# Three seven-product pairs as third, fifth and seventh of eight, a bank emptied twice, and banks that swap in odd blocks

## The chip, the cores and the metric

The kernel runs on one core of a Trainium2 chip. The time is device microseconds of one execution of the whole program; lower is better. In the profile PE is TensorE's matmuls, PEld its weight loads, DVE is VectorE, ACT is ScalarE, POOL is GpSimd, and SP issues most of the DMAs.

## What is computed

Two transformer-like blocks run on 256 tokens of width 2048, in float32. The changed part is the feed-forward half of the first block: a normalised input is multiplied by a matrix of 2048 x 11264 whose left half gives `g` and whose right half gives `u`, and `silu(g) * u` is multiplied by a matrix of 5632 x 2048.

```python
h2 = _rmsnorm(x, ffn_norm_w[l])
g, u = jnp.split(jnp.einsum('bsd,df->bsf', h2, w_gate_up[l]), 2, axis=-1)
x = x + jnp.einsum('bsf,fd->bsd', jax.nn.silu(g) * u, w_down[l])
```

## The kernel before

**Three matmuls for one product.** Every float32 operand is split into a high and a low part of a shorter float type (`parts_of` for weights: ScalarE writes `wh`, VectorE writes `wl = raw - wh`). `tri` (L642) makes a product from three matmuls of 128x128 by 128x512 at L645, L646 and L647: high by high, high by low, low by high.

**Blocks and pairs.** `hidden_pre(f, ...)` works on one block f of 512 columns of `g` and the 512 columns of `u` that belong to it; there are 11 blocks, done in parts of 4, 4 and 3, and each part is followed by its share of the down product (`proj(gu, w_down, ...)`, matmuls at L166 to L168). Inside a block the 2048 rows of the weight are eight pairs p of 2 x 128 rows. The tokens are two tiles of 128, so a pair is a 2x2 by 2x2 product of tiles (tokens by rows, rows by `g`/`u`). A *plain* pair makes its eight products. A *seven-product* pair makes seven, from sums of tiles: the sums of the inputs (`F`, four of them) are made once, by `seven_forms`, for the pairs in `sums7`; the sums of the weights (`Ta`, `Tb`) are made by VectorE for each block and pair (L687 to L691), and they are split like the weights. Before the change the pairs 2, 4 and 7 are of this kind.

**Banks.** There are eight banks for matmul results. Five are the pool `pmm` (tile name p in the profile, `mm_bank`), three are the pool `phd` (tile name h, `bank`). A block holds all eight: P1, P2, P5, P6, P7 in `pmm` and P3, P4, X4 in `phd`. Plain pairs write P2, P4 (the `g` half, two token tiles), P3 and X4 (the `u` half). Seven-product pairs write P1, P2, P5, P7, P6, P4 and P3, in that order. X4 gets nothing from a seven-product pair, so before the last pair it is copied out (`x4`, L679), and `before_last` runs the *turn* of the previous block in it: eight transposes (L735) that turn the previous block's hidden values, in two halves of four, each read by ScalarE and VectorE (`unit_split`). A pool gives its buffers in rotation: the tile asked for next waits until the readers of the one that had the buffer are done.

**Emptying.** After the last pair the seven banks are combined (L715 to L723): `s1` is a copy of P1; then eight additions on VectorE, of which each reads at most one bank. Two Silu on ScalarE and two multiplications on VectorE (`hd`, L725 and L726) end the block.

**Loads and order.** A load is 512 KB (`load`, L115), issued by SP into the ring of `raw` buffers, two pools of four used in turn. `Ta` and `Tb` are taken from the same ring. Split weights live in six buffer pairs (`more_w`). The framework sorts the instructions of each engine beforehand, by readiness and priority; loads, splits, weight sums and the emptying have a raised priority (`tc.high_priority`). At run time each engine goes through its list in order. So a block's matmuls don't stand in the list in the order of the source.

Of the kernel before, what the change touches and what calls it, by code (L numbers as in the profile page):

```python
# [8 lines left out]
F32 = mybir.dt.float32  # L9
# [4 lines left out]
ALU = mybir.AluOpType  # L14
# [5 lines left out]
NT = 2  # L20
CW = 512
# [8 lines left out]
def tile_two_blocks(  # L30
# [19 lines left out]
    def stt(out, in0, scalar, in1, op0, op1):  # L50
        nc.vector.scalar_tensor_tensor(out=out, in0=in0, scalar=scalar, in1=in1, op0=op0, op1=op1)  # L51

    def tt(out, a, b, op):
        nc.vector.tensor_tensor(out=out, in0=a, in1=b, op=op)  # L54
# [7 lines left out]
    def act(out, in_, func=AF.Copy, **kw):  # L62
        nc.scalar.activation(out=out, in_=in_, func=func, **kw)  # L63
# [4 lines left out]
    def bank(shape):  # L68
        return phd.tile(shape, F32, tag="h", name="h")
# [38 lines left out]
    def raw_tile(nk, n):  # L108
        raw = (more_raw[-1] if more_raw else wraw).tile([128, nk, n], F32, tag="raw", name="raw")
        more_raw.reverse()  # L110
        return raw

    def load(w, r0, nk, c0, n):
        raw = raw_tile(nk, n)
        nc.sync.dma_start(  # L115
            out=raw, in_=w[r0:r0 + nk * 128, c0:c0 + n].rearrange("(k p) n -> p k n", p=128)
        )
        return raw

    def parts_of(raw, pool=None):  # L120
        if pool is None:
            pool = more_w[0] if more_w else wsp
            if more_w:
                more_w.append(more_w.pop(0))
        wh = pool.tile(list(raw.shape), F32R, tag="wh", name="wh")
        wl = pool.tile(list(raw.shape), F32R, tag="wl", name="wl")
        act(wh, raw)
        tt(wl, raw, wh.bitcast(F32), ALU.subtract)
        return wh, wl

    def split(w, r0, nk, c0, n, pool=None):
        with tc.high_priority(4000):
            return parts_of(load(w, r0, nk, c0, n), pool)

    def mm_bank():
        return pmm.tile([128, CW], F32, tag="p", name="p")
# [6 lines left out]
    def ordered(a):  # L143
        return a.rearrange("p (b h) -> p h b", h=2)

    def two(a):
        return a.rearrange("p (h b) -> p h b", h=2)
# [122 lines left out]
    def col(name, k):  # L270
        o = off[name] + k
        return cm[:, o:o + 1]
# [328 lines left out]
    fp = ff.enter_context(tc.tile_pool(name="fp", bufs=1))  # L601
    sums7 = {}

    def seven_forms(c):

        def keep(j, ps):
            p = 2 * c + j
            if p not in (2, 4, 7):
                return
            x_ = fp.tile([128, CW], F32, tag="s1", name="xs").rearrange("p (a t) -> p a t", a=2)  # L610
            for a in range(2):
                act(x_[:, a], ps[:, a], scale=col("ffn", 2 * p + a))
            (a11, a21), (a12, a22) = ((x_[:, a, :128], x_[:, a, 128:]) for a in range(2))
            s_ = fp.tile([128, CW], F32, tag="u2", name="ss").rearrange("p (i t) -> p i t", i=4)
            tt(s_[:, 0], a21, a22, ALU.add)
            tt(s_[:, 1], s_[:, 0], a11, ALU.subtract)
            tt(s_[:, 2], a11, a21, ALU.subtract)
            tt(s_[:, 3], a12, s_[:, 1], ALU.subtract)
            F = fp.tile([128, 4, 2, 128], F32R, tag=f"F{p}", name=f"F{p}")
            act(F[:, :, 0], s_)  # L620
            tt(F[:, :, 1], s_, F[:, :, 0].bitcast(F32), ALU.subtract)
            sums7[p] = F
        return keep
# [18 lines left out]
    def tri(pt, left, right, st, sp):  # L642
        (xh, xl), (wh, wl) = left, right
        mh, ml = in_turn(wh), in_turn(wl)
        nc.tensor.matmul(pt, lhsT=xh, rhs=mh, start=st, stop=False)  # L645
        nc.tensor.matmul(pt, lhsT=xh, rhs=ml, start=False, stop=False)  # L646
        nc.tensor.matmul(pt, lhsT=xl, rhs=mh, start=False, stop=sp)  # L647

    def hidden_pre(f, before_last):

        P1, P2, P6, P7, P5 = [mm_bank() for i in range(5)]
        P3, P4, X4 = [bank([128, CW]) for i in range(3)]
        begun = set()
        order = [0, 1, 2, 3, 4, 5, 6, 7]
        last_plain = max(p for p in order if p not in sums7)

        def prod(pt, left, right, end=False):
            tri(pt, left, right, id(pt) not in begun, end)
            begun.add(id(pt))

        for p in order:
            u, a0 = x1u[p // 2], 2 * (p % 2)
            r0, end = 256 * p, p == order[-1]

            def x_(a, t):
                sl = slice(t * 128, (t + 1) * 128)
                return u[:, a0 + a, 0, sl], u[:, a0 + a, 1, sl]

            if p not in sums7:
                for (b0, b1), c0 in (((P2, P4), f * CW), ((P3, X4), DFF + f * CW)):  # L670
                    wh, wl = split(w_gate_up, r0, 2, c0, CW)
                    for a in range(2):
                        for t, b in enumerate((b0, b1)):
                            prod(b, x_(a, t), (wh[:, a], wl[:, a]), b is X4 and p == last_plain and a == 1)
                continue
            if end:
                x4 = fp.tile([128, CW], F32, tag="x4", name="x4")
                with tc.high_priority(4000):
                    act(x4, X4)  # L679
                before_last(X4)  # L680
            F = sums7[p]
            with tc.high_priority(4000):
                g_ = load(w_gate_up, r0, 2, f * CW, CW)
                u_ = load(w_gate_up, r0, 2, DFF + f * CW, CW)
                B1 = parts_of(g_)
                Ta, Tb = raw_tile(2, CW), raw_tile(2, CW)
                tt(Ta[:, 0], u_[:, 0], g_[:, 0], ALU.subtract)  # L687
                tt(Ta[:, 1], u_[:, 1], u_[:, 0], ALU.subtract)
                W13 = parts_of(Ta)
                tt(Tb[:, 0], u_[:, 1], Ta[:, 0], ALU.subtract)  # L690
                tt(Tb[:, 1], g_[:, 1], Tb[:, 0], ALU.subtract)  # L691
                W24 = parts_of(Tb)
                B22 = parts_of(u_[:, 1:2])

            def at(w, a):
                return w[0][:, a], w[1][:, a]

            def form(i):
                return F[:, i, 0], F[:, i, 1]

            prod(P1, x_(0, 0), at(B1, 0), end)
            prod(P2, x_(1, 0), at(B1, 1), end)
            prod(P5, form(0), at(W13, 0), end)
            prod(P7, form(2), at(W13, 1), end)
            prod(P6, form(1), at(W24, 0), end)
            prod(P4, x_(1, 1), at(W24, 1), end)
            prod(P3, form(3), at(B22, 0), end)

        s1 = fp.tile([128, CW], F32, tag="s1", name="s1")
        u2 = fp.tile([128, CW], F32, tag="u2", name="u2")  # L710
        u3 = fp.tile([128, CW], F32, tag="u3", name="u3")
        g = fp.tile([128, NT, CW], F32, tag="g", name="g")
        h = fp.tile([128, NT, CW], F32, tag="hd", name="hd", bufs=2)
        with tc.high_priority(4000):
            act(s1, P1)  # L715
            tt(g[:, 0], P2, s1, ALU.add)
            tt(u2, P6, s1, ALU.add)
            tt(u3, P7, u2, ALU.add)
            tt(g[:, 1], P4, u3, ALU.add)
            tt(u2, P5, u2, ALU.add)  # L720
            tt(u3, P5, u3, ALU.add)
            tt(u2, P3, u2, ALU.add)
            tt(u3, u3, x4, ALU.add)  # L723
        for t, up_ in enumerate((u2, u3)):
            act(g[:, t], g[:, t], AF.Silu, scale=rs1[:, t:t + 1])  # L725
            stt(two(h[:, t]), ordered(up_), rs1[:, t:t + 1], ordered(g[:, t]), ALU.mult, ALU.mult)  # L726
        return h
# [16 lines left out]
    for part in (range(0, 4), range(4, 8), range(8, 11)):  # L744
        gu = []
        waiting = lambda ps: None
        for f in part:
            h = hidden_pre(f, waiting)
            gu.append((new_unit(), f * CW))
            waiting = turn(h, gu[-1][0])  # L750
        waiting(bank([128, CW]))
        for c in range(4):
            residual(proj(gu, w_down, c * CW), c)
            if part[-1] == 10:
                x2u.append(unit_from(xk(c), lambda k, c=c: wfg[:, 4 * c + k:4 * c + k + 1]))
                stats_piece(st, xc(c), c)
# [294 lines left out]
    for t in range(NT):  # L1051
        sl = slice(t * 128, (t + 1) * 128)
        n = CW if t == 0 else CW // 2
# [64 lines left out]
```

## Time and profile before

| | us |
|---|---|
| median of three executions | 1635.47 |
| lowest, highest | 1633.23, 1636.78 |
| the profiled execution | 1633.28 |
| its span | 1631.5 |
| gate/up blocks and down product, first to last matmul | about 523 to 1227 |

Matmul rows overlap: the time of a row is longer than the distance to the next one. So a stall is read from the distance between starts, or by counting matmuls in a window. Transposes of the turn are the rows `h<-ident,hd`; the products of a seven-product pair that use a sum of inputs are the rows with `F` among their operands; in the emptying the names are `s` (`s1`), `u` (`u2`, `u3`), `g` and `x` (`x4`).

### The profile page before, as it was taken

What the parts mean: (1) busy time and instruction counts of PE and PEld (TensorE: products, weight loads), DVE (VectorE), ACT (ScalarE), POOL (GpSimd) and SP (SyncE); (2) the same over time, 40 slices, a digit from 0 to 9 for tenths busy, and PEclk for the clock granted to TensorE, in tenths of its full rate; (3) what the DMA queues carried; (4) which work ended last, traced back from release to release, by engine and by line L of the source; (5) the groups of instructions that cost most, each with busy time, mean ns of one, the idle gap of its engine ahead of it and who ended that gap; (6) DMA issues with size and microseconds to landing.
All of it is one profiled execution on the core that took longest, in us unless ns stands there. A gap on an engine that the chain in (4) does not pass through costs nothing.

```text
span 1631.5 us, 22403 instructions
## 1 busy us (share of the span) xinstructions
PE 1596.9 (98%) x8433; PEld 1410.5 (86%) x8433; DVE 1238.2 (76%) x1715; ACT 885.5 (54%) x1156; POOL 23.6 (1%) x57
## 2 busy tenths in 40 slices
PE   8999999999999999999999999998999999999998
PEld 7999999999988888788887788887889888998987
DVE  7769768765667798875699875688877899766854
ACT  5657557544555555554455554455545455655743
POOL 3000000000000000000000000000000000000000
PEclk9999999999999999999999999999999999999999
DMA  8764565466686566675665576465856566556564
GB/s 291 216 196 153 156 191 168 146 191 197 218 285 204 169 201 189 210 248 171 195 197 185 186 251 209 147 201 184 261 170 186 176 182 218 183 166 192 159 216 143
DMA packets 166892, 318.36 MB, mean 195 GB/s; under 512 B 12248, under 2 KB 13168, under 8 KB 166784
## 3 DMA queue, kind: packets, MB, share of 16 engines
q1 hardware_dynamic: 164304, 312.19, 61.2%
q10 hardware_dynamic: 2032, 4.60, 0.8%
q8 instruction: 66, 1.08, 0.3%
q0 software_dynamic: 448, 0.14, 0.1%
q14 instruction: 42, 0.34, 0.1%
HBM read 313.74 MB, written 3.15 MB: 194 GB/s over the span
## 4 chain that ended last, share of the span: by engine, by line
PE 77%; DVE 14%; DMA 4%; issue 3%; ACT 1%; DVEq 0%; ACTq 0%; POOLq 0%; POOL 0%
PE p L194 18%; PE p L167 10%; PE p L168 10%; PE p L166 10%; PE p L195 9%; DVE wl L54 8%; DMA raw<-in_w_gate_up_dram 4%; PE h L646 3%; PE h L647 3%; PE h L645 3%; DVE raw L54 2%; PE h L446 2%; PE p L646 2%; PE p L647 1%; PE p L645 1%
## 5 line engine op out<-in xcount | busy, mean ns | idle before, releaser
L63 ACT ACTIVATE wh<-raw 128x1024 fp32r<-128x1024 f32 (+1 forms) x646 | 655.8, 1031 | 586.3 <-PE p L168 176.4
L54 DVE TENSOR_TENSOR wl<-raw,wh 128x1024 fp32r<-128x1024 f32 (+1 forms) x646 | 756.8, 1188 | 273.4 <-ACT wh L63 269.1
L194 PE MATMUL p<-u,wh 128*128 128x512 f32 x1392 | 458.7, 383 | 0.6 <-DVE sg L54 0.6
L195 PE MATMUL p<-u,wl 128*128 128x256 f32 x1392 | 365.6, 274 | 1.0 <-DVE wl L54 0.9
L167 PE MATMUL p<-wl,u 128*128 128x512 f32 x832 | 317.0, 382 | 0.9 <-DVE wl L54 0.9
L168 PE MATMUL p<-wh,u 128*128 128x512 f32 x832 | 312.6, 381 | 2.0 <-DVE u L51 2.0
L166 PE MATMUL p<-wh,u 128*128 128x512 f32 x832 | 311.8, 381 | 1.1 <-ACT u L63 0.6
L194 PEld LDWEIGHTS p<-u,wh 128*128 128x128 f32 x1392 | 260.1, 190 | 31.3 <-DVE sg L54 1.1
L195 PEld LDWEIGHTS p<-u,wl 128*128 128x128 f32 x1392 | 266.5, 191 | 8.4 <-DVE wl L54 1.7
L166 PEld LDWEIGHTS p<-wh,u 128*128 128x128 f32 x832 | 157.0, 189 | 23.2 <-ACT u L63 1.4
L168 PEld LDWEIGHTS p<-wh,u 128*128 128x128 f32 x832 | 156.5, 189 | 23.5 <-DVE u L51 2.8
L167 PEld LDWEIGHTS p<-wl,u 128*128 128x128 f32 x832 | 157.3, 189 | 22.6 <-DVE wl L54 1.3
L646 PE MATMUL h<-wl,u 128*128 128x512 f32 x363 | 138.0, 380 | 0.1
L647 PE MATMUL h<-wh,u 128*128 128x512 f32 x363 | 137.1, 379 | 0.0
L645 PE MATMUL h<-wh,u 128*128 128x512 f32 x363 | 135.3, 381 | 0.0
L54 DVE TENSOR_TENSOR raw<-raw 128x512 f32<-128x512 f32 x132 | 87.2, 685 | 56.6 <-DMA raw<-in_w_gate_up_dram 55.7
L646 PE MATMUL p<-wl,u 128*128 128x512 f32 x176 | 69.1, 392 | 10.8 <-DVE wl L54 10.7
L646 PEld LDWEIGHTS h<-wl,u 128*128 128x128 f32 x363 | 68.6, 189 | 10.7 <-DVE wl L54 1.2
L645 PEld LDWEIGHTS h<-wh,u 128*128 128x128 f32 x363 | 68.6, 189 | 10.1 <-DVE u L54 0.7
L647 PEld LDWEIGHTS h<-wh,u 128*128 128x128 f32 x363 | 68.6, 189 | 9.6
L645 PE MATMUL p<-wh,u 128*128 128x512 f32 x176 | 65.8, 385 | 3.2 <-DVE g L54 3.2
L647 PE MATMUL p<-wh,u 128*128 128x512 f32 x176 | 67.3, 382 | 0.0
(298 smaller groups left out, 1483.6 us busy)
## 6 DMA issues: line engine op xcount, KB each, us to landing
raw<-in_w_in_dram SPq DMA_DIRECT2D x232, 512.0 KB, 4.0
raw<-in_w_gate_up_dram SPq DMA_DIRECT2D x176, 512.0 KB, 4.5
raw<-in_w_down_dram SPq DMA_DIRECT2D x88, 512.0 KB, 5.1
raw<-in_w_out_dram SPq DMA_DIRECT2D x64, 512.0 KB, 4.9
raw<-in_w_mem_kv_dram SPq DMA_DIRECT2D x14, 512.0 KB, 5.7
xp<-in_x_dram SPq DMA_DIRECT2D x4, 512.0 KB, 6.6
X<-in_x_dram SPq DMA_DIRECT2D x4, 512.0 KB, 6.1
mp<-in_mem_dram SPq DMA_DIRECT2D x3, 512.0 KB, 7.6
```

What stands on the lines that cost most here:

```text
L54: nc.vector.tensor_tensor(out=out, in0=a, in1=b, op=op)
L63: nc.scalar.activation(out=out, in_=in_, func=func, **kw)
L166: nc.tensor.matmul(pt[t], lhsT=u[:, k, 0, sl], rhs=mh, start=st, stop=False)
L167: nc.tensor.matmul(pt[t], lhsT=u[:, k, 0, sl], rhs=ml, start=False, stop=False)
L168: nc.tensor.matmul(pt[t], lhsT=u[:, k, 1, sl], rhs=mh, start=False, stop=sp)
L194: nc.tensor.matmul(pt[f], lhsT=wh[:, a, fs], rhs=both, start=st, stop=False)
L195: nc.tensor.matmul(pt[f][:, :T], lhsT=wl[:, a, fs], rhs=high, start=False, stop=False)
L446: nc.tensor.matmul(ps[:, h], lhsT=k[:, h, s * 128:(s + 1) * 128], rhs=q[:, h, t * 128:(t + 1) * 128], start=True, stop=True,)
L645: nc.tensor.matmul(pt, lhsT=xh, rhs=mh, start=st, stop=False)
L646: nc.tensor.matmul(pt, lhsT=xh, rhs=ml, start=False, stop=False)
L647: nc.tensor.matmul(pt, lhsT=xl, rhs=mh, start=False, stop=sp)
```

## The change

The seven-product pairs become 2, 4 and 6, and pair 7 is plain. P1, P5, P6 and P7 get their last product in pair 6, the other four banks in pair 7. X4 is copied out after pair 5 (the last plain pair before 7), the turn runs in it there, and pair 7 opens it anew, so that it is emptied a second time at the end, by an addition to `x4`. The emptying has nine additions; P1 is copied into `g[:, 0]`, and `s1` is gone. In odd blocks the pools change: P2, P1, P4, P3, X4 are the five of `pmm` and P6, P7, P5 the three of `phd`; because of the rotation, the four banks that a block opens first are those of P1, P6, P7, P5 of the block before. `Ta` and `Tb` are buffers of their own, one each, no longer of the raw ring. `hd` has one buffer instead of two, and the input sums are made in the buffer of `u3`.

```diff
-            if p not in (2, 4, 7):
+            if p not in (2, 4, 6):
                 return
-            x_ = fp.tile([128, CW], F32, tag="s1", name="xs").rearrange("p (a t) -> p a t", a=2)
+            x_ = fp.tile([128, CW], F32, tag="u3", name="xs").rearrange("p (a t) -> p a t", a=2)
...
-    def hidden_pre(f, before_last):
-
-        P1, P2, P6, P7, P5 = [mm_bank() for i in range(5)]
-        P3, P4, X4 = [bank([128, CW]) for i in range(3)]
+    def hidden_pre(f, between):
+
+        five, three = [mm_bank() for i in range(5)], [bank([128, CW]) for i in range(3)]
+        if f % 2:
+            P2, P1, P4, P3, X4 = five
+            P6, P7, P5 = three
+        else:
+            P1, P2, P6, P7, P5 = five
+            P3, P4, X4 = three
         begun = set()
-        order = [0, 1, 2, 3, 4, 5, 6, 7]
-        last_plain = max(p for p in order if p not in sums7)
...
-                            prod(b, x_(a, t), (wh[:, a], wl[:, a]), b is X4 and p == last_plain and a == 1)
+                            prod(b, x_(a, t), (wh[:, a], wl[:, a]), a == 1 and (end or (b is X4 and p == 5)))
+                if p == 5:
+                    x4 = fp.tile([128, CW], F32, tag="x4", name="x4")
+                    with tc.high_priority(4000):
+                        act(x4, X4)
+                    between(X4)
+                    begun.discard(id(X4))
                 continue
-            if end:
-                x4 = fp.tile([128, CW], F32, tag="x4", name="x4")
-                with tc.high_priority(4000):
-                    act(x4, X4)
-                before_last(X4)
...
-                Ta, Tb = raw_tile(2, CW), raw_tile(2, CW)
+                Ta, Tb = (fp.tile([128, 2, CW], F32, tag=n, name=n) for n in ("Ta", "Tb"))
...
-            prod(P1, x_(0, 0), at(B1, 0), end)
-            prod(P2, x_(1, 0), at(B1, 1), end)
-            prod(P5, form(0), at(W13, 0), end)
-            prod(P7, form(2), at(W13, 1), end)
-            prod(P6, form(1), at(W24, 0), end)
-            prod(P4, x_(1, 1), at(W24, 1), end)
-            prod(P3, form(3), at(B22, 0), end)
-
-        s1 = fp.tile([128, CW], F32, tag="s1", name="s1")
+            prod(P1, x_(0, 0), at(B1, 0), p == 6)
+            prod(P2, x_(1, 0), at(B1, 1))
+            prod(P5, form(0), at(W13, 0), p == 6)
+            prod(P7, form(2), at(W13, 1), p == 6)
+            prod(P6, form(1), at(W24, 0), p == 6)
+            prod(P4, x_(1, 1), at(W24, 1))
+            prod(P3, form(3), at(B22, 0))
+
...
-        h = fp.tile([128, NT, CW], F32, tag="hd", name="hd", bufs=2)
+        h = fp.tile([128, NT, CW], F32, tag="hd", name="hd")
         with tc.high_priority(4000):
-            act(s1, P1)
-            tt(g[:, 0], P2, s1, ALU.add)
-            tt(u2, P6, s1, ALU.add)
+            act(g[:, 0], P1)
+            tt(u2, P6, g[:, 0], ALU.add)
             tt(u3, P7, u2, ALU.add)
+            tt(g[:, 0], P2, g[:, 0], ALU.add)
+            tt(x4, x4, u3, ALU.add)
             tt(g[:, 1], P4, u3, ALU.add)
+            tt(x4, P5, x4, ALU.add)
             tt(u2, P5, u2, ALU.add)
-            tt(u3, P5, u3, ALU.add)
+            tt(x4, X4, x4, ALU.add)
             tt(u2, P3, u2, ALU.add)
-            tt(u3, u3, x4, ALU.add)
-        for t, up_ in enumerate((u2, u3)):
+        for t, up_ in enumerate((u2, x4)):
```

More of the change, by code (lines that the diff above doesn't have):

```diff
@@ L659, in prod @@
             begun.add(id(pt))
-        for p in order:
+        for p in range(8):
             u, a0 = x1u[p // 2], 2 * (p % 2)
-            r0, end = 256 * p, p == order[-1]
+            r0, end = 256 * p, p == 7
             def x_(a, t):
```

## The prediction

> **What bounds the kernel now.** I read the page first (busy times, the chain), then the source view of the product lines, then windows over the gate/up stage, and last the timelines of PE, DVE and ACT around one border between two column blocks.
>
> ```profile
> PE 1596.9 (98%) x8433; PEld 1410.5 (86%) x8433; DVE 1238.2 (76%) x1715; ACT 885.5 (54%) x1156; POOL 23.6 (1%) x57
> PE 77%; DVE 14%; DMA 4%; issue 3%; ACT 1%; DVEq 0%; ACTq 0%; POOLq 0%; POOL 0%
> ```
>
> TensorE is nearly always occupied, and only what shortens its stream or fills its holes can count. The second line says where holes come from: 14% of the chain is VectorE, 4% is DMA.
>
> How many products the changed stage has stands in the source view of L645, the first of the three matmuls that every product issues (L645, L646, L647):
>
> ```profile
> L645 PE MATMUL h<-wh,u x363: 379/379/484, 526.0 to 1160.2; 128*128 128x512 f32 x182
> L645 PE MATMUL p<-wh,u x176: 379/379/634, 523.2 to 1157.6; 128*128 128x512 f32 x176
> L645 PE MATMUL p<-wh,F x99: 379/379/634, 529.7 to 1159.6; 128*128 128x512 f32 x99
> L645 PE MATMUL h<-wh,F x33: 379/379/379, 541.2 to 1160.9; 128*128 128x512 f32 x33
> ```
>
> 363 + 176 + 99 + 33 = 671 products, 61 for each of the 11 blocks f: five plain pairs of 8 and three seven-product pairs of 7. That is 183 matmuls per block. The 379 ns are not their price, since they overlap; the price is the distance of starts. Here is PE at the border of f=1 and f=2:
>
> ```profile
> 607.18 0.60 PE L735 MATMUL h<-ident,hd 128*128 128x128 f32 x4
> 607.53 0.46 PE L645 MATMUL p<-wh,u 128*128 128x512 f32 x1
> 607.83 0.38 PE L646 MATMUL p<-wl,u 128*128 128x512 f32 x1
> ...
> 608.91 0.38 PE L645 MATMUL p<-wh,u 128*128 128x512 f32 x1
> 611.02 0.48 PE L646 MATMUL p<-wl,u 128*128 128x512 f32 x1 [1.73 <-DVE wl L54]
> 611.34 0.38 PE L647 MATMUL p<-wh,u 128*128 128x512 f32 x1
> 611.56 0.38 PE L645 MATMUL p<-wh,u 128*128 128x512 f32 x1
> 611.77 0.38 PE L646 MATMUL p<-wl,u 128*128 128x512 f32 x1
> ...
> 616.59 0.60 PE L735 MATMUL h<-ident,hd 128*128 128x128 f32 x4
> 616.95 0.46 PE L645 MATMUL h<-wh,u 128*128 128x512 f32 x1
> ```
>
> Undisturbed starts are 0.216 us apart (611.34, 611.56, 611.77). Four transposes cost 607.83 - 607.18 less one step, 0.43 us. A block with its turn of the previous block (8 transposes) therefore needs 183 x 0.216 + 0.87 = 40.4 us. Measured between two turns:
>
> ```profile
> 607.18:651.76 44.58, 41.80 (x193) 34.96 (x192) 38.81 (x47) 24.30 (x28) 0.00 (x0) 1.00 0.61 189
> 651.76:696.14 44.38, 41.72 (x193) 35.01 (x192) 39.75 (x47) 24.72 (x29) 0.00 (x0) 1.00 0.69 218
> 860.36:906.32 45.96, 43.48 (x193) 36.02 (x191) 39.70 (x48) 23.97 (x28) 0.00 (x0) 0.96 0.59 183
> 906.32:950.84 44.52, 41.45 (x192) 35.11 (x191) 40.23 (x47) 24.68 (x29) 0.00 (x0) 1.00 0.71 224
> 1114.91:1161.52 46.61, 42.03 (x193) 34.96 (x192) 41.56 (x49) 24.38 (x29) 0.00 (x0) 1.00 0.67 213
> 866.00:869.00 3.00, 3.00 (x8) 2.14 (x7) 3.00 (x5) 0.56 (x2) 0.00 (x0) 0.50 0.83 246
> ```
>
> (Columns: window, length, busy PE, PEld, DVE, ACT, POOL, granted clock, DMA.) The five periods exceed 40.4 by 4.2, 4.0, 5.6, 4.1 and 6.2 us: 24.1 us. About 1.5 of the third is a dip of the clock to 0.50 (last row).
>
> The whole stage by counting matmuls, and one stretch of the down product for comparison:
>
> ```profile
> 523.20:696.40 173.20, 165.46 (x760) 139.59 (x760) 148.71 (x185) 97.97 (x115) 1.61 (x1) 1.00 0.62 196
> 696.40:784.40 88.00, 88.00 (x417) 77.08 (x415) 57.65 (x61) 39.25 (x40) 0.00 (x0) 1.00 0.63 200
> 784.40:951.00 166.60, 160.87 (x734) 136.98 (x734) 141.17 (x165) 91.95 (x106) 0.00 (x0) 0.99 0.63 199
> 1040.00:1161.90 121.90, 117.22 (x542) 100.33 (x540) 102.01 (x118) 67.70 (x77) 0.00 (x0) 1.00 0.65 203
> ```
>
> Taking out the transposes (28, 20 and 12 at 0.11), 732, 714 and 530 steps of 0.216 leave 12.0, 10.2 and 6.1 us over, 28 us in all; the down product leaves nothing. So **28 us is the most that this change can win**: 24 in the five periods, some 4 at the first block and the three first borders.
>
> Why the border stalls is in the first PE fence. From 607.53 to 616.59 PE writes only p banks: P2 of pairs 0 and 1 and P1, P2, P5, P7, P6 of pair 2, which is 9 products or 27 matmuls, 5.8 us of work in 9.1 us. The h banks, which hold P3, P4 and X4, are shut, and this is who shuts them:
>
> ```profile
> 609.15 0.68 DVE L54 TENSOR_TENSOR g<-p,s 128x512 f32<-128x512 f32 x1
> 609.75 1.21 DVE L54 TENSOR_TENSOR wl<-raw,wh 128x1024 fp32r<-128x1024 f32 x1
> 610.89 0.68 DVE L54 TENSOR_TENSOR u<-p,s 128x512 f32<-128x512 f32 x1
> ...
> 615.49 0.68 DVE L54 TENSOR_TENSOR u<-h,u 128x512 fp32r<-128x512 f32 x1
> 616.09 0.68 DVE L54 TENSOR_TENSOR g<-h,u 128x512 f32<-128x512 f32 x1
> ...
> 619.84 0.68 DVE L54 TENSOR_TENSOR u<-h,u 128x512 f32<-128x512 f32 x1
> ...
> 621.57 0.68 DVE L54 TENSOR_TENSOR u<-h,u 128x512 fp32r<-128x512 f32 x1
> ```
>
> P4 is emptied at 616.09 (`g<-h,u`), and at 616.95 PE's first product into an h bank starts. P3 follows at 619.84, X4 at 621.57, when the turn's second half is read. The emptying steps take turns with weight splits, one each per 1.74 us (609.15 to 610.89). The wait of 1.73 us that the trace books on `wl` follows from this: PE, with one bank of four, eats a split pair in a third of the usual time.
>
> **The change, part by part.** Matmul, split and load counts stay (three seven-product pairs, now 2, 4, 6). The prices of what moves:
>
> ```profile
> L54 DVE TENSOR_TENSOR wl<-raw,wh 128x1024 fp32r<-128x1024 f32 x272 | 326.1, 1218 | 70.2 <-ACT wh L63 67.0 <-DMA raw<-in_w_down_dram 2.4
> L54 DVE TENSOR_TENSOR raw<-raw 128x512 f32<-128x512 f32 x128 | 84.5, 685 | 55.0 <-DMA raw<-in_w_gate_up_dram 54.0 <-issue 0.4
> L51 DVE SCALAR_TENSOR_TENSOR hd<-u,rs,g 128x512 f32<-128x512 f32 x20 | 18.4, 919 | 0.0
> ```
>
> *Pair 7 plain, banks swapped.* P1, P5, P6, P7 now close in pair 6, and 24 matmuls (5.2 us) of pair 7 follow. The next block has its P2, P4, P3, X4 where P1, P7, P6, P5 were. ACT's copy and the first two VectorE steps of the new order free P1, P6 and P7; P5's last read is the 7th VectorE step. At one step per 1.74 us, starting 1.3 us before pair 6 ends, that is 10.9 us after its end, while the new X4 is first wanted 15 matmuls into the next block, 5.2 + 3.2 = 8.4 us after. It may be 2.5 us late; P2, P4 and P3 of pair 1 (18 matmuls, 3.9 us) can go ahead. So the 3.3 us lost on banks at a border go. Left over is what weights cost: from pair 7 to pair 2 VectorE has 3 x 2 splits of 1.22, a seven-product pair (3 x 1.22 and a half-sized split and four weight sums at 0.69 = 7.1), nine steps of emptying and two `hd` writes (9 x 0.68 + 2 x 0.92 = 8.0): 22.4 us against 3 x 5.2 + 4.5 = 20.1 us of PE. A lead of 2.3 us is eaten, and six split buffers hold more. I keep **1 us of stall per period**, between 0 and the present 4.2.
>
> *One more VectorE step.* Nine additions take the place of eight: 0.68 us per block (`u<-p,s` above). VectorE's 38.8 busy us of a 44.58 us period become 39.5, still under 40.4, so it costs nothing by itself while VectorE isn't idle for other reasons; if that cover fails it is 11 x 0.68 = 7.5 us.
>
> *Ta and Tb out of the raw ring.* Of 22 raw allocations per block 6 go; the eight slots then hold half a block's 16 loads, 20 us ahead instead of 14.7. In the groups above VectorE waited 54.0 us in all for gate/up loads, most of its 5.8 us idle per period. I expect most of that gone. The single Ta must have been read before it is written again, two pairs (45 matmuls, 9.7 us) later: nothing, and one ACT read of about a microsecond if that cover is gone.
>
> *The eighth bank twice.* After pair 5 ACT copies X4, the turn of the previous block runs in it, and pair 7 opens it anew. X4 is wanted 21 + 15 matmuls after pair 5, 7.8 us. The turn now takes, from its first transposes to its last read, 622.25 - 607.18 = 15.1 us, but its steps alone (two times 0.6 + 0.6 + 0.7) some 4. Half of those 15 us were ACT's queue:
>
> ```profile
> 602.84 0.60 ACT L63 ACTIVATE x<-h 128x512 f32<-128x512 f32 x1 [0.45 <-PE h L647]
> ...
> 609.87 0.72 ACT L63 ACTIVATE g<-g,rs 128x512 f32<-128x512 f32 x1 [3.11 <-DVE g L54]
> ...
> 612.39 0.58 ACT L63 ACTIVATE u<-h 128x512 fp32r<-128x512 f32 x1
> ```
>
> its `u<-h` stood behind a Silu (609.87) that had waited 3.11 us for `g`. That Silu now comes after the turn. I take no stall, with both ends kept below as a rival.
>
> *The rest* (`hd` single, `s1` gone, pair 6's form made one transpose earlier): each has its old reader done long before; nothing, bounded by one step of 0.7 us per block.
>
> **Sum.** Five periods: 24.1 less 5 kept = 19. First borders: 2 of 4. That makes 21, of which I leave 1 for a startup at the first block that the change doesn't touch: 20. The profiled execution took 1633.3 us (span 1631.5), 2.2 under the median of 1635.47; by the median, **1615 us**.
>
> [...]
>
> **The rivals.**
> - *VectorE sets the pace.* If its idle time is only halved, a period is 39.5 + 2.9 = 42.4 us. The five take 212 us in place of 226, 14 won; the first blocks of the three parts each pay the extra step too (about 2) and their borders give nothing: 12, **1624 us**. For it: busy 38.8 to 41.6 per period above. Against: 54 us of its waits are loads.
> - *No change.* PE's order is not the source order (the trace moves P2 of pairs 0 to 2 forward), and banks freed late by the 1.74 us rhythm keep the border as it is: **1635 us**.
> - *Slower: the turn keeps X4 shut in pair 7.* If it still takes 15.1 us from pair 6's end, X4's 6 matmuls, wanted 3.2 us later, are 11.9 us late. P2, P4, P3 of the next pair 0 cover 3.9. The other 8 us stall in each of the 8 blocks with a turn: 64 less the 28 won, **1671 us**; it decides from a stall of 28 / 8 = 3.5 us per block. Against it: ACT's queue is clear there. The Trainium skill (PSUM — Partial Sum Buffer, § PSUM bank collisions raise a hardware error) forbids two engines on one bank at a time, so each of X4's hand-overs (PE, ACT, PE, ACT, VectorE, twice, then PE) is a wait. The trace shows just such waits at 615.49 and 616.59.
>
> **How the numbers follow.** Forecast 0.62 (own range 1606 to 1622); VectorE's pace 0.17; no change 0.09; slower 0.12. A measurement of this kernel tells 0.2% (3.3 us) from no change. Faster: 0.62 + 0.17 + 0.02 of the third = 0.81; same 0.08; slower 0.11. The range takes the first two, 1606 to 1630, and leaves a little over 0.2 out.
>
> **What would show it.** Right: periods of 41 to 42 us between turns; after pair 7 PE writes four different banks at once; VectorE's wait for gate/up loads well under 54 us; both halves of the turn before pair 7's last 9 matmuls. Wrong: periods near 44 with PE waiting for `wl` (VectorE's pace), or PE waiting behind the transposes of L735's successor (X4).

## The result and the profile after

The changed kernel took 1613.12 us in the median of four runs (1612.46 to 1613.91), the kernel before 1635.18 us beside it: a ratio of 0.9866, 95% interval 0.9849 to 0.9883. The forecast was 1615. **The number came out, and the reason given for it did not**, as the experiments show.

The page of the changed kernel, its busy times and its chain:

```profile
PE 1591.7 (99%) x8433; PEld 1411.7 (88%) x8433; DVE 1245.7 (77%) x1726; ACT 886.4 (55%) x1156; POOL 23.1 (1%) x57
PE 77%; DVE 16%; issue 4%; DMA 3%; ACT 1%; ACTq 0%; DVEq 0%; POOLq 0%; POOL 0%
```

As many matmuls as before, and eleven more VectorE instructions, one per block. The periods between turns, in windows of the changed kernel (length, then busy time of PE, PEld, DVE, ACT, POOL with the number of instructions in brackets, granted clock, DMA share, GB/s):

```profile
599.42:642.34 42.92, 42.14 (x196) 35.53 (x194) 39.73 (x49) 24.51 (x30) 0.00 (x0) 1.00 0.63 198
642.34:681.52 39.18, 37.88 (x178) 32.52 (x177) 39.11 (x47) 21.76 (x26) 0.00 (x0) 1.00 0.61 189
847.32:889.80 42.48, 41.73 (x194) 35.04 (x192) 38.89 (x49) 24.10 (x29) 0.00 (x0) 1.00 0.60 187
889.80:929.54 39.74, 38.54 (x182) 33.21 (x181) 39.70 (x47) 22.48 (x27) 0.00 (x0) 1.00 0.66 201
1095.33:1137.12 41.79, 41.18 (x193) 35.32 (x192) 40.69 (x49) 24.08 (x29) 0.00 (x0) 1.00 0.63 200
```

The periods differ because the turn doesn't stand at the same place among the products: 196 and 178 matmuls in the first two, where each period before had 192 or 193. The five sum to 206.1 us against 226.1 before, but they hold 943 matmuls against 964, and 21 x 0.216 = 4.5 us of the difference is work that lies elsewhere. So the stall left is 206.1 - (202 - 4.5) = 8.6 us, 1.7 per period, against 24.1 us before.

The border of f=1 and f=2, now on PE:

```profile
599.42 0.60 PE L739 MATMUL p<-ident,hd 128*128 128x128 f32 x4
...
604.12 0.48 PE L646 MATMUL p<-wl,u 128*128 128x512 f32 x1 [0.18 <-DVE wl L54]
...
605.08 0.38 PE L645 MATMUL h<-wh,u 128*128 128x512 f32 x1
...
609.89 0.60 PE L739 MATMUL p<-ident,hd 128*128 128x128 f32 x4
...
616.85 0.38 PE L645 MATMUL p<-wh,u 128*128 128x512 f32 x1
```

In this odd block its own P2, P4, P3 and X4 are p banks. At 605.08 PE goes on to products in h banks, those of the next block, before the turn's second half has run (609.89). VectorE's last read of the turn is the second of the two instructions merged in this row, over at 615.85, 16.4 us after the turn began:

```profile
614.56 1.29 DVE L54 TENSOR_TENSOR u<-p,u 128x512 f32<-128x512 f32 x2
```

Only then can X4's products of pair 7 start, the p products at 616.85. So the long turn of the slower rival did come, and in this block it cost nearly nothing: PE had other products to make.

What VectorE waits for, by releaser, in the window 523 to 1162, changed kernel:

```profile
DVE wl L54 <- ACT wh L63: 69.2, 63, 1.9
DVE Ta L54 <- DMA raw<-in_w_gate_up_dram: 27.7, 10, 3.6
```

54.0 us for gate/up loads have become 27.7. That looked like a companion of the gain. The experiments show it to be the main source.

### The profile page after: what moved, and what is told of

Read it like the earlier page. It is cut to its first block, busy times and chain, and to the rows that moved or that the text cites. A ratio compares the mean times of both kernels' runs of the same rounds, so it can differ in the third digit from the quotient of the medians.

```text
span 1611.9 us, 22433 instructions
## 1 busy us (share of the span) xinstructions
PE 1591.7 (99%) x8433; PEld 1411.7 (88%) x8433; DVE 1245.7 (77%) x1726; ACT 886.4 (55%) x1156; POOL 23.1 (1%) x57
## 4 chain that ended last, share of the span: by engine, by line
PE 77%; DVE 16%; issue 4%; DMA 3%; ACT 1%; ACTq 0%; DVEq 0%; POOLq 0%; POOL 0%
PE p L194 18%; PE p L167 11%; PE p L168 11%; PE p L166 11%; PE p L195 9%; DVE wl L54 8%; DMA raw<-in_w_gate_up_dram 2%; PE h L446 2%; PE p L646 2%; PE p L647 2%; PE p L645 2%; DVE Tb L54 1%; PE h L646 1%; PE h L647 1%; PE h L645 1%
## 5 line engine op out<-in xcount | busy, mean ns | idle before, releaser
L54 DVE TENSOR_TENSOR wl<-raw,wh 128x1024 fp32r<-128x1024 f32 (+1 forms) x580 | 685.0, 1193 | 269.0 <-ACT wh L63 265.8
L63 ACT ACTIVATE wh<-raw 128x1024 fp32r<-128x1024 f32 (+1 forms) x580 | 589.6, 1029 | 516.5 <-PE p L168 169.8
L167 PE MATMUL p<-wl,u 128*128 128x512 f32 x832 | 318.0, 383 | 0.9 <-DVE wl L54 0.9
L166 PE MATMUL p<-wh,u 128*128 128x512 f32 x832 | 313.3, 381 | 1.7 <-ACT u L63 1.2
L168 PE MATMUL p<-wh,u 128*128 128x512 f32 x832 | 313.6, 382 | 0.7 <-DVE u L51 0.7
L166 PEld LDWEIGHTS p<-wh,u 128*128 128x128 f32 x832 | 157.2, 189 | 24.1 <-ACT u L63 2.0
L167 PEld LDWEIGHTS p<-wl,u 128*128 128x128 f32 x832 | 157.5, 189 | 22.7 <-DVE wl L54 1.3
L168 PEld LDWEIGHTS p<-wh,u 128*128 128x128 f32 x832 | 157.0, 190 | 22.1 <-DVE u L51 1.3
L646 PE MATMUL p<-wl,u 128*128 128x512 f32 x341 | 130.1, 383 | 2.3 <-DVE wl L54 2.3
L647 PE MATMUL p<-wh,u 128*128 128x512 f32 x341 | 128.3, 379 | 0.0
L645 PE MATMUL p<-wh,u 128*128 128x512 f32 x341 | 123.7, 380 | 0.0
L646 PE MATMUL h<-wl,u 128*128 128x512 f32 x198 | 75.4, 381 | 2.0 <-DVE wl L54 2.0
L646 PEld LDWEIGHTS p<-wl,u 128*128 128x128 f32 x341 | 64.4, 189 | 14.3 <-DVE wl L54 5.6
L647 PE MATMUL h<-wh,u 128*128 128x512 f32 x198 | 75.1, 379 | 0.0
L645 PE MATMUL h<-wh,u 128*128 128x512 f32 x198 | 74.6, 382 | 0.3 <-DVE u L54 0.2
L645 PEld LDWEIGHTS p<-wh,u 128*128 128x128 f32 x341 | 64.5, 189 | 9.0
L647 PEld LDWEIGHTS p<-wh,u 128*128 128x128 f32 x341 | 64.5, 189 | 8.7
L54 DVE TENSOR_TENSOR Ta<-raw 128x512 f32<-128x512 f32 x66 | 42.8, 694 | 29.7 <-DMA raw<-in_w_gate_up_dram 29.5
```

The source lines that it names most:

```text
L166: nc.tensor.matmul(pt[t], lhsT=u[:, k, 0, sl], rhs=mh, start=st, stop=False)
L167: nc.tensor.matmul(pt[t], lhsT=u[:, k, 0, sl], rhs=ml, start=False, stop=False)
L168: nc.tensor.matmul(pt[t], lhsT=u[:, k, 1, sl], rhs=mh, start=False, stop=sp)
```

## The experiments

The ratios are to the kernel before, in runs on the same chip.

**e1: Ta and Tb back in the raw ring, the rest of the change kept.**

```diff
-                Ta, Tb = (fp.tile([128, 2, CW], F32, tag=n, name=n) for n in ("Ta", "Tb"))
+                Ta, Tb = raw_tile(2, CW), raw_tile(2, CW)
```

> The changed kernel with Ta and Tb taken from the raw ring again. If banks carry the gain (theory): 1613 to 1618 us, periods between turns still near 41 us, though VectorE's wait for gate/up loads goes back from 27.7 to some 50 us. If late loads carried it (rival): 1624 us or more, with periods of 43 us.

Measured 1631.47 us, ratio 0.9983 (0.9975 to 0.9992). The wait for gate/up loads is 52.3 us again, and nearly all of the gain is gone: the swap and the new order of pairs together are worth 3.0 us. The theory of the prediction falls, and the rival that I had set against it here holds.

**e2: the changed kernel without the swap.**

```diff
-        if f % 2:
+        if False:
```

> The changed kernel without the swap: every block has P1, P2, P6, P7, P5 in the five and P3, P4, X4 in the three. Theory (the swap lets the next block start): a block's P2, P4, P3 and X4 wait for the same banks of the block before, so 1620 to 1630 us and a hole at each border. Rival (the plain last pair and the loads do it, the swap is decoration): 1616 us or less.

Measured 1621.92 us, ratio 0.9923 (0.9910 to 0.9937), as the theory of this expectation said. Inside this order of pairs the swap is worth 8.8 us. Without it, waits for banks are visible on PE:

```profile
PE h L645 <- DVE g L54: 6.0, 6, 1.1
```

**e3: the kernel before with Ta and Tb apart, and nothing else of the change but what makes room for them.**

```diff
...
-                Ta, Tb = raw_tile(2, CW), raw_tile(2, CW)
+                Ta, Tb = (fp.tile([128, 2, CW], F32, tag=n, name=n) for n in ("Ta", "Tb"))
...
-        h = fp.tile([128, NT, CW], F32, tag="hd", name="hd", bufs=2)
+        h = fp.tile([128, NT, CW], F32, tag="hd", name="hd")
...
-            act(s1, P1)
-            tt(g[:, 0], P2, s1, ALU.add)
-            tt(u2, P6, s1, ALU.add)
+            act(g[:, 0], P1)
+            tt(u2, P6, g[:, 0], ALU.add)
+            tt(g[:, 0], P2, g[:, 0], ALU.add)
```

> The kernel before with only Ta and Tb out of the raw ring (and, to find the room, one hd buffer and P1 copied into g instead of s1). Theory: banks still shut the border, 1630 to 1636 us, while VectorE's wait for gate/up loads halves. Rival (loads): 1624 us or less.

Measured 1607.58 us, ratio 0.9837 (0.9823 to 0.9850): **faster than the whole change**, by one part of it. The expectation was wrong, and its trace says why. The same border on PE in e3:

```profile
603.29 0.60 PE L734 MATMUL h<-ident,hd 128*128 128x128 f32 x4
...
609.20 0.38 PE L647 MATMUL p<-wh,F 128*128 128x512 f32 x1
609.41 0.60 PE L734 MATMUL h<-ident,hd 128*128 128x128 f32 x4
609.77 0.46 PE L645 MATMUL h<-wh,u 128*128 128x512 f32 x1
```

The order is that of before: transposes, 24 matmuls in p banks alone, transposes, the first product in an h bank. The work in it is 0.43 + 24 x 0.216 = 5.6 us. Before, it took 616.59 - 607.18 = 9.41 us; here 6.12. PE keeps to one kind of bank as long as it did, in number of products, and that costs 0.5 us in place of 3.8. VectorE's rows show the difference. Before, at the borders of f=0, f=1 and f=9 (the first, second and last of eight):

```profile
563.27 1.90 DVE L54 TENSOR_TENSOR raw<-raw 128x512 f32<-128x512 f32 x3 [4.34 <-DMA raw<-in_w_gate_up_dram]
604.47 1.90 DVE L54 TENSOR_TENSOR raw<-raw 128x512 f32<-128x512 f32 x3 [3.25 <-DMA raw<-in_w_gate_up_dram]
1113.80 1.29 DVE L54 TENSOR_TENSOR raw<-raw 128x512 f32<-128x512 f32 x2 [4.31 <-DMA raw<-in_w_gate_up_dram]
```

and e3 at f=1:

```profile
597.11 0.69 DVE L54 TENSOR_TENSOR Ta<-raw 128x512 f32<-128x512 f32 x1 [1.42 <-DMA raw<-in_w_gate_up_dram]
...
608.91 0.68 DVE L54 TENSOR_TENSOR g<-h,u 128x512 f32<-128x512 f32 x1
```

Before, VectorE stands still for 3.25 us ahead of weight sums (by their place those of the next block's pair 2, since pair 7's products are running by then), and all behind them in its list is late: the splits that PE wants at 611.02, the emptying, the turn. The 3.8 us that PE loses between the transposes are in the main that wait, passed on. In e3 the wait is shorter and comes earlier; P4 is emptied at 608.91, and PE's first h product starts at 609.77. From the first transposes until P4 is read out it is 9.6 us before and 6.3 in e3: the banks are shut 3.3 us less.

**e4: the kernel before with only the swap** (the `if f % 2` of the change put into `hidden_pre`, all else as before).

> The kernel before with only the swap of banks in odd blocks; pairs 2, 4 and 7 and the old emptying. P1, P7, P6, P5 close in the last pair, so their banks come free one VectorE step at a time, but none waits for the turn. Theory: half of the gain, 1620 to 1629 us. Rival (the swap alone is the change): 1612 to 1617 us.

Measured 1627.62 us, ratio 0.9964 (0.9951 to 0.9976). The swap alone wins 6 to 7 us, about a third of the 19 that I had put down to banks, and inside the range that I had expected for it.

**e6: e3's changes that make room, but with Ta and Tb in the ring** (e3's diff without the two lines of `Ta, Tb`).

> The kernel before with only what made room in the Ta/Tb run: one hd buffer, P1 copied into g in place of s1, input sums in u3's buffer; Ta and Tb stay in the raw ring. New theory (late loads put VectorE in debt, and the debt keeps banks shut): no gain, 1632 to 1637 us, VectorE's wait for gate/up loads near 54 us. Rival (the order of emptying was the gain of that run): 1612 us or less.

Measured 1633.56 us, ratio 0.9990 (0.9980 to 1.0000), with 53.1 us of waiting for gate/up loads: as the new theory said, the room-makers are not the gain.

**e7 and e11: e3 with six and with seven load buffers.**

```diff
-    more_raw.extend([wraw, ff.enter_context(tc.tile_pool(name="wraw2", bufs=4))])
+    w2 = ff.enter_context(tc.tile_pool(name="wraw2", bufs=2))
+    more_raw.extend([wraw, w2, wraw])
```

(with `raw_tile` taking the pools of that list in turn; e11 has `bufs=3` and `[wraw, w2, wraw, w2, wraw, w2, wraw]`).

> The Ta/Tb-apart kernel with six load buffers (wraw, wraw2, wraw in turn, wraw2 with two) instead of eight. In the kernel before the loads had 16 of 22 turns in eight buffers, as many as 5.8. If depth of look-ahead is what counts: most of the gain is lost, 1624 us or more, the wait for gate/up loads 45 us or more. If it counts that a load no longer stands behind a sum's readers: 1607 to 1613 us.

> The Ta/Tb-apart kernel with seven load buffers (wraw four, wraw2 three, in turn). Six gave 1644 us, eight 1608 us. If the depth of the look-ahead is what counts, seven lies between: 1615 to 1632 us, with VectorE's wait for gate/up loads between 46.2 and 21.1 us. If six was bad for a reason of its own (the order of the two pools): 1607 to 1612 us.

Measured 1644.27 us (ratio 1.0057, 1.0044 to 1.0071) with six and 1618.00 us (0.9900, 0.9887 to 0.9914) with seven; eight gave 1607.58. VectorE's wait for gate/up loads, six buffers and then seven:

```profile
DVE Ta L54 <- DMA raw<-in_w_gate_up_dram: 46.2, 21, 4.8
DVE Ta L54 <- DMA raw<-in_w_gate_up_dram: 38.6, 22, 3.8
```

and 21.1 with eight. The depth of the look-ahead is what counts, and both times lie in the ranges expected for that: 26 us for the seventh, 10 for the eighth. The wait is no exact measure of the time: six buffers waited less than the kernel before (46.2 against 54.0) and were slower. Nor is the count of buffers: by the share of turns the kernel before had 5.8, yet it beat six by 9 us. Why is open.

**e8: e3 and the swap.**

> The Ta/Tb-apart kernel with the swap of banks in odd blocks as well, pairs 2, 4, 7. If banks are shut only through VectorE's debt, the swap has nothing left to win: 1605 to 1609 us. If banks still cost: 1603 us or less.

Measured 1605.11 us, ratio 0.9814 (0.9800 to 0.9827): the fastest kernel that ran, in the old order of pairs. With VectorE on time the swap wins 2.5 us by the medians, 3.7 by the ratios: little, as the first half of the expectation said.

**e9: e3 with a ninth addition; e13: the changed kernel with a tenth and an eleventh.**

```diff
             tt(u3, u3, x4, ALU.add)
+            tt(x4, x4, x4, ALU.add)
```

(e13 adds `tt(u3, u3, u3, ALU.add)` twice after the last addition of the changed kernel.)

> The Ta/Tb-apart kernel with one more addition per block on VectorE at the end of the emptying (x4 added to itself, its value no longer used), so as many VectorE steps as the changed kernel. If the ninth step is what the changed kernel lost against the Ta/Tb-apart kernel: 1612 to 1615 us (11 x 0.68 = 7.5 us at most). If the order of the pairs lost it: 1607 to 1609 us.

> The changed kernel with two more VectorE additions per block at the end of the emptying (u3 added to itself, value not used). One more step cost the Ta/Tb-apart kernel 2.4 us. If VectorE's load prices the changed kernel in the same way: 1617 to 1620 us. If the changed kernel is nearer to VectorE's pace: 1622 to 1628 us (22 x 0.68 = 15 us at most). If the steps are hidden: 1613 to 1615 us.

Measured 1609.99 us (0.9846, 0.9833 to 0.9860) and 1615.55 us (0.9890, 0.9874 to 0.9906): 2.4 us for one step more per block in e3, 2.4 us for two in the changed kernel (1.5 and 3.9 by the ratios). A step is mostly hidden, but not free. Both times fell between the ranges expected, above "hidden" and below the full price.

**e10: e8 with one weight sum per pair on GpSimd.**

```diff
-                tt(Ta[:, 1], u_[:, 1], u_[:, 0], ALU.subtract)
+                nc.gpsimd.tensor_tensor(out=Ta[:, 1], in0=u_[:, 1], in1=u_[:, 0], op=ALU.subtract)
```

> The kernel with Ta and Tb apart and the swap, pairs 2, 4, 7, and one of the four weight sums of a pair (Ta's second half) on GpSimd in place of VectorE: 33 steps of 0.69 us leave VectorE, 2.1 us per block. If VectorE's load still sets what little stall is left: 1601 to 1604 us. If that stall is late loads and start of the first block: 1604 to 1607 us. If the sum on GpSimd comes late, W13 with it: 1608 us or more.

Measured 1607.69 us, ratio 0.9844 (0.9830 to 0.9857): 2.6 us worse than e8, and between the second and the third range expected. In the groups of e10 the sum takes 1.70 us on GpSimd, and VectorE's next sum, which reads what GpSimd reads beside it, has grown:

```profile
L693 POOL TENSOR_TENSOR Ta<-raw 128x512 f32<-128x512 f32 x33 | 56.2, 1702 | 559.0 <-DMA raw<-in_w_gate_up_dram 440.4 <-DVE wl L54 118.6
L54 DVE TENSOR_TENSOR Tb<-raw,Ta 128x512 f32<-128x512 f32 x32 | 28.7, 896 | 0.4
```

The same sum in e8:

```profile
L54 DVE TENSOR_TENSOR Tb<-raw,Ta 128x512 f32<-128x512 f32 x32 | 22.0, 688 | 0.1
```

The mean of 896 ns in e10 mixes two cases: of the 32 sums 25 took 0.68 or 0.69 us and 7 took 1.65 or 1.66, such as this one, which runs beside GpSimd's:

```profile
599.28 1.82 POOL L693 TENSOR_TENSOR Ta<-raw 128x512 f32<-128x512 f32 x1 [11.38 <-DMA raw<-in_w_gate_up_dram]
600.00 1.65 DVE L54 TENSOR_TENSOR Tb<-raw,Ta 128x512 f32<-128x512 f32 x1
```

It ends at 601.65, 0.55 us after GpSimd's sum (601.10). The Trainium skill (SBUF — State Buffer, § SBUF: two separate sides) says that a VectorE instruction with two SBUF inputs and a GpSimd instruction that reads SBUF exclude each other for their whole length. These rows agree with that. Other weight sums and splits of VectorE grew as well, so that its busy time didn't fall, with 33 instructions fewer (e8, then e10):

```profile
PE 1587.9 (99%) x8433; PEld 1413.5 (88%) x8433; DVE 1239.7 (77%) x1715; ACT 888.9 (55%) x1156; POOL 22.7 (1%) x57
PE 1588.8 (99%) x8433; PEld 1413.0 (88%) x8433; DVE 1243.1 (77%) x1682; ACT 889.2 (55%) x1156; POOL 78.6 (5%) x90
```

So e10 doesn't tell what a lighter VectorE would win. Which of the two, the growth or the later sum, cost the 2.6 us was not taken apart.

**e12: the changed kernel with neither Ta and Tb apart nor the swap** (the diffs of e1 and e2 together): the new order of pairs by itself.

> The changed kernel with neither Ta and Tb apart nor the swap, so the new order of pairs (2, 4, 6, a plain last pair, X4 emptied twice, nine steps) alone. If the new order costs by itself, as the two Ta/Tb-apart kernels without swap say (1622 against 1608 us): 1637 to 1650 us, slower than before. If the order is neutral and only went badly with the deeper ring: 1631 to 1637 us.

Measured 1646.95 us, ratio 1.0085 (1.0071 to 1.0099). The new order alone is slower than the kernel before, as the first half of the expectation said.

## Why the prediction was right, and where it was wrong

The eight combinations of the three parts, in us. They come from several sets of runs, between which the kernel before lay at 1633.3 to 1635.6, so a difference under 2 us says little. The right column holds the ninth step and the room-makers as well, and so do e3 and e8 the room-makers (e6: about nothing):

| | pairs 2, 4, 7 | pairs 2, 4, 6, plain last |
|---|---|---|
| Ta, Tb in the ring, no swap | 1634.5 (before) | 1646.95 (e12) |
| Ta, Tb in the ring, swap | 1627.62 (e4) | 1631.47 (e1) |
| Ta, Tb apart, no swap | 1607.58 (e3) | 1621.92 (e2) |
| Ta, Tb apart, swap | 1605.11 (e8) | 1613.12 (after) |

Read down, Ta and Tb apart win 18 to 27 us in each of the four pairs of cells. The swap wins 2.5 to 15.5. Read across, the new order costs 4 to 14.

- **What could be won.** The count of 28 us over the matmuls, 24 of it in the five periods, stood: the profiled execution of e8, with as many matmuls, is 28.2 us shorter than the one before (1605.11 and 1633.28). The changed kernel left 8.6 us in the periods, for which I had kept 5, and so won 15.5 there, not 19. The sum of 20 came to 22.1 by the medians; the rest lies outside the five periods, where the sum had 1 us, and was not taken apart.
- **The step that failed is "why the border stalls".** I saw PE write one kind of bank for 9.1 us, found the other banks shut, and wrote that the wait on `wl` followed from it. (I also counted nine products there; the rows hold eight, 24 matmuls, so that the loss is 3.8 us and not 3.3.) It was the other way round. e3 has the same sequence with the same banks and 0.5 us of stall. The `wl` was late because VectorE had waited 3.25 us for a load, one border after the other; the banks were shut long because the emptying stood behind the same wait.
- **So the terms had the wrong owners.** "The 3.3 us lost on banks at a border go" was booked on the swap and the plain last pair. "Ta and Tb out of the raw ring" was booked at nothing, though the 54.0 us of waiting were in the row quoted. By the table that term is 27 us in the old order and 18 in the changed kernel, and the swap and the plain last pair, which had all the rest, are worth 3.0 together (e1). That 3 and 18 added up to nearly the 20 of the sum is luck. The argument of 16 loads in eight buffers against 22 allocations was the right one, and was left out of the sum.
- **The swap** is worth 6 to 7 us alone and 2.5 once loads are early, not 19. **The new order**, for which I had "no stall", costs 12 to 14 us without the swap and 4 to 8 with it. In it the banks that a block closes last are those that the next one opens first (the 6.0 us in e2), unless they are swapped. Why it costs 8 us even with the swap is not settled; the ninth addition is about 1 to 2 of it, and the changed kernel still has one load wait at each of the eight borders, 1.9 to 3.6 us, as at f=0 and f=9:

```profile
557.92 1.29 DVE L54 TENSOR_TENSOR Ta<-raw 128x512 f32<-128x512 f32 x2 [3.04 <-DMA raw<-in_w_gate_up_dram]
1094.25 1.29 DVE L54 TENSOR_TENSOR Ta<-raw 128x512 f32<-128x512 f32 x2 [3.55 <-DMA raw<-in_w_gate_up_dram]
```

  Before, these waits were 3.3 to 4.7 us at each of the eight. So these waits became shorter, 24.7 us in all against 33.9, and did not go; the waits for gate/up loads elsewhere fell from 20.1 to 3.0. How much of the gain is due to either was not taken apart.
- **The eighth bank.** That the turn would be short because "ACT's queue is clear there" was wrong: it still takes some 16 us. For the first half ACT's queue was clear, and VectorE read 8 us later, in its place in its list:

```profile
600.59 0.58 ACT L63 ACTIVATE u<-p 128x512 fp32r<-128x512 f32 x1
608.58 0.69 DVE L54 TENSOR_TENSOR u<-p,u 128x512 fp32r<-128x512 f32 x1
```

  That it cost little is due to the next block's products in swapped banks, which in the block shown covered more than the 3.9 us that I had counted. The rows at 615.49 and 616.59, quoted for waits on a shared bank, show none: VectorE was busy with splits until the first, and PE with matmuls until the second.
- **One more VectorE step** was put at nothing and costs 1.2 to 2.4 us over the kernel, near the noise between sets.
- **VectorE's pace**, as a rival, was near the truth in kind: VectorE's lateness did set the border. But it was idle, not overloaded: it waited for loads.
- Open: each kernel also gets another list of instructions from the framework's sorting, and differences of 2 or 3 us may be due to that.

## What to carry to other kernels

Before a stall is put down to the resource that is shut, follow the engine that should open it back to its own idle time: a wait of 3 us upstream is passed on from engine to engine and shows up under another name. A ring of load buffers that also lends buffers to computed tiles is shallower than its count; near the limit one buffer more or less was worth 10 to 26 us of 1610. And a forecast that lands on the number has tested nothing about its parts: undo each part alone, since here one part won more than the whole and another lost.

## What the runs showed of the hardware

A subtraction of two 128x512 float32 tiles from SBUF took 1.70 us on GpSimd in the mean, at the least 1.27, and 0.69 on VectorE, and VectorE subtractions of the same shape that ran beside it took 1.65 us in 7 of 32 cases. The clock's dip to 0.50 after a border stall, seen in one of five periods before, is not among the five periods of the changed kernel, whose granted clock is 1.00 in each.
